# Splitting x from a turned host copy, with the first norm's row factor put on the projections

## The chip, the cores and the metric

One core of a Trainium2 chip runs the whole program. The time is the device time of one execution in microseconds (us), taken as the median of several runs. Engines: PE multiplies matrices into PSUM, DVE (VectorE), ACT (ScalarE) and POOL (GpSimd) do elementwise work, SP issues transfers. Each works through its own list of instructions in order and waits at semaphores.

## The reference, cut to what matters

Two sequences of 512 tokens (1024 tokens, D_MODEL 1024) go through one encoder layer. The first norm and the projections that read it are what is changed:

```python
def rms_norm(x, g):
    y = xf * lax.rsqrt(jnp.mean(xf * xf, axis=-1, keepdims=True) + EPS)
    return (y * g).astype(x.dtype)

h = rms_norm(x, ln1_gain)
q, k, v, u, g_attn, g_ssm = split(h @ w_in)      # six projections
```

u (1024 columns) goes into the state-space branch: blocks of 8 steps, 64 groups of 16 channels, a scan over 64 chunks in both directions. g_attn and g_ssm (1024 columns each) are gates and pass a sigmoid. q and k pass a norm over each head of 64 (q * rsqrt(mean q^2 + EPS)) and go, with v, into a windowed attention. An MLP follows. The row factor rsqrt(mean x^2 + EPS) is one number for each token, the gain is one number for each of the 1024 input columns.

All arithmetic is fp32. A product of two fp32 operands is made as three PE products: each operand is split into a high part (ACT rounds it to the PE's fp32r) and a low part (DVE subtracts), and hi*hi, hi*lo and lo*hi are added in PSUM.

## The kernel before, in words

The normed x is held as hT: for each sequence (of two, index s) a tile of 128 partitions (columns of x within a block) x 8 blocks k x 512 tokens, high and low part (the tiles act). To make it, the front loads x by rows, 8 tiles `xt` of 128 tokens x 1024 columns; ACT squares a tile with a sum over its row (L297), POOL adds EPS and takes the power -0.5, DVE multiplies the row tile by that factor (L303, 8 instructions of 128x1024). For each (s, k) PE turns four 128x128 pieces into one PSUM bank (L308), ACT writes the high part times the gain from that bank, DVE the low part (L311).

**Columns.** The 24 blocks of 128 columns (8 u, 8 g_attn, 8 g_ssm) each have a weight of 128x8x128, loaded by SP in halves (c_raw) one block ahead and split by ACT (c_hi, L175) and DVE (c_lo, L176). A block makes two *products*, one for each sequence: 24 matmuls of 128x512 into one of three PSUM banks (acc, L185). ACT then takes the bank into a tile of both sequences (128x1024, tag ev, two buffers): u with a rearrangement, gates by a sigmoid (L202), or by a copy late in the program. ACT's queue stores the tile to DRAM (u_scr, ga_scr, gs_scr). Then follow 8 key products (L225), normed at once, which stay in two ev tiles and are moved to the attention's tile kn by two transfers.

**Fillers.** All these products come from one generator. The other stages call pull(units) and thereby put the next matmuls of the generator into the PE order between their own (a matmul counts 2 units, one of a key product 1). The order of each engine is thus written out by hand in the front and the tables, and for PE, ACT and DVE in the later stages too; there POOL and SP are ordered by a scheduler. What a stage pulls is the same before and after except in the front.

**Stages in order.** The *front*: x, its split, the first products, and some hundred small DVE instructions on 128x64 tiles (exponentials and sines for the step sizes). The *tables*: for 16 quarters, DVE builds tables of powers, PE turns them (L524) and multiplies them with u and with each other (L553), while columns are pulled. Sums of lags go to lag_scr. The *scan*: 62 steps on DVE, four instructions of 128x256 each on two SBUF operands (L621 to L624), pull(15) after each. The *states*: after the scan 128 groups of PE products on u and on the Toeplitz blocks (L655) and on the states, in 8 batches whose operands (u_sb, toep, ctab) POOL's queue loads. toep comes from toep_scr, which POOL's queue fills from lag_scr by 8 transfers (L595) before the scan. Then keys, gated linear unit, attention, output product, MLP.

The lines most spoken of:

```python
V.tensor_mul(t1, h[:, i], a8r)              # a step of the scan, L621 to L624
V.tensor_mul(t2, h[:, i, ::-1], a8i)
V.tensor_add(t1, t1, h[:, i + 1])
V.tensor_add(h[:, i + 1], t1, t2)
pull(15)
```

## Time and profile before

| | us |
|---|---|
| three runs | 1472.97, 1475.15, 1476.32 (median 1475.15) |
| span of the profiled execution | 1471.1 |
| first turn of a table (end of the front) | 55.84 |
| first step of the scan on DVE | 213.13 |
| last step of the scan on DVE | 324.21 |
| states end, keys begin | 404.50 |
| PE busy | 1442.0 (98%) |
| DVE busy | 1092.2 (74%) |
| ACT busy | 754.9 (51%) |
| POOL busy | 226.8 (15%) |

The first column of a row in the chain of waits or in a timeline is the time in us at which the work began, the second how long it took. A group of instructions is shown as line, engine, operation, output<-inputs, shape, count, then the busy time in us and the mean of one in ns, then the idle time ahead of it and what ended most of it. Where a line's instructions are listed with three figures (270/272/421) these are the shortest, the middle and the longest in ns, followed by the time from the first to the last. The stages show DVE in turn as the fuller or the emptier neighbour of PE, so each is read by itself.

### The profile page before, as it was taken

To read this page: it belongs to the slowest core of one execution; us is meant where nothing else is said; L and a number is where in the kernel's file an instruction comes from. 1 tells how busy PE (TensorE), PEld (TensorE's weight loads), DVE (VectorE), ACT (ScalarE), POOL (GpSimd) and SP (SyncE) were. 2 spreads that over 40 slices of the span, in tenths; PEclk is the share of its full clock that TensorE was granted. 3 is DMA by queue.
4 is the path that set the end of the run, shared out by engine and by line. 5 is a ranking of instruction groups with operands and counts; after the bars stand their busy time and mean duration, and the time that the engine had idled before them with its cause. 6 is when DMAs were issued, how large, how long until landed. Compare 5 with 4: busy or idle time off the path is not lost.

```text
span 1471.1 us, 22069 instructions
## 1 busy us (share of the span) xinstructions
PE 1442.0 (98%) x8074; PEld 1230.7 (84%) x8074; DVE 1092.2 (74%) x1965; ACT 754.9 (51%) x1346; POOL 226.8 (15%) x372
## 2 busy tenths in 40 slices
PE   6999999999999999999999999999999999999998
PEld 4888888888999999987888878888888878888787
DVE  7989849995446899988985587777776597475553
ACT  6678852234336888786343355454454444333332
POOL 3044451003332442252100000000000000000000
PEclk9999999999999999999999999999999999999999
DMA  4455559428630533345552255444442993454441
GB/s 177 137 165 174 159 157 339 144 100 288 234 135 24 172 104 106 105 150 177 182 192 102 86 169 174 149 146 154 145 146 108 339 330 103 158 184 147 126 130 58
DMA packets 98269, 234.48 MB, mean 159 GB/s; under 512 B 11722, under 2 KB 23242, under 8 KB 98160
## 3 DMA queue, kind: packets, MB, share of 16 engines
q1 hardware_dynamic: 59088, 135.35, 28.5%
q0 software_dynamic: 15744, 47.23, 9.9%
q10 hardware_dynamic: 23328, 50.47, 9.4%
q8 instruction: 64, 1.05, 0.3%
q14 instruction: 45, 0.37, 0.1%
HBM read 163.78 MB, written 80.77 MB: 166 GB/s over the span
## 4 chain that ended last, share of the span: by engine, by line
PE 74%; DVE 12%; DMA 4%; issue 4%; ACT 4%; POOL 2%; SPq 0%; DVEq 0%; ACTq 0%; POOLq 0%
PE bank L117 14%; PE bank L118 13%; PE bank L116 13%; PE acc L185 6%; PE acc L821 5%; PE acc L117 3%; PE acc L118 3%; PE acc L116 3%; PE acc L123 2%; DMA c_raw<-in_w_ug_dram 2%; PE sps L553 2%; PE po L904 2%; PE sps L872 2%; PE tps L888 2%; PE acc L225 1%
## 5 line engine op out<-in xcount | busy, mean ns | idle before, releaser
L185 PE MATMUL acc<-act,c_hi 128*128 128x512 f32 x768 | 244.2, 396 | 1.0 <-DVE act L311 1.0
L117 PE MATMUL bank<-b_lo,a_hi 128*128 128x512 f32 x448 | 174.6, 390 | 2.3 <-DVE b_lo L1515 2.3
L118 PE MATMUL bank<-b_hi,a_lo 128*128 128x512 f32 x448 | 174.3, 389 | 0.0
L116 PE MATMUL bank<-b_hi,a_hi 128*128 128x512 f32 x448 | 173.5, 389 | 0.0
L185 PEld LDWEIGHTS acc<-act,c_hi 128*128 128x128 f32 x768 | 143.0, 189 | 30.4 <-DVE act L311 2.4
L1514 ACT CAST a_hi<-d_a 128x1024 fp32r<-128x1024 f32 x56 | 59.0, 1054 | 180.5 <-PE bank L117 177.1
L185 PE MATMUL acc<-act,c_lo 128*128 128x512 f32 x384 | 151.0, 393 | 0.0
L116 PE MATMUL bank<-act,act 128*128 128x512 f32 x368 | 143.3, 389 | 0.5 <-ACT f_sum L1339 0.5
L117 PE MATMUL bank<-act,act 128*128 128x512 f32 x368 | 143.3, 389 | 0.2 <-DVE act L1298 0.2
L118 PE MATMUL bank<-act,act 128*128 128x512 f32 x368 | 143.2, 389 | 0.0
L1515 DVE TENSOR_TENSOR a_lo<-d_a,a_hi 128x1024 fp32r<-128x1024 f32 x56 | 68.5, 1224 | 98.5 <-ACT a_hi L1514 98.5
L821 PE MATMUL acc<-w_hi,act 128*128 128x256 f32 x512 | 114.1, 291 | 0.0
L117 PEld LDWEIGHTS bank<-b_lo,a_hi 128*128 128x128 f32 x448 | 84.1, 188 | 20.7 <-DVE b_lo L1515 3.3
L116 PEld LDWEIGHTS bank<-b_hi,a_hi 128*128 128x128 f32 x448 | 84.1, 188 | 17.6
L118 PEld LDWEIGHTS bank<-b_hi,a_lo 128*128 128x128 f32 x448 | 84.1, 188 | 17.4
L821 PEld LDWEIGHTS acc<-w_hi,act 128*128 128x128 f32 x512 | 87.1, 190 | 3.7
L185 PEld LDWEIGHTS acc<-act,c_lo 128*128 128x128 f32 x384 | 72.3, 188 | 14.7 <-DVE c_lo L176 0.4
L882 ACT ACTIVATE p<-p,nmx 128x257 f32<-128x257 f32 (+1 forms) x128 | 72.1, 564 | 19.7 <-DVE nmx L876 17.6
L116 PEld LDWEIGHTS bank<-act,act 128*128 128x128 f32 x368 | 69.1, 188 | 15.4 <-ACT f_sum L1339 0.9
L117 PEld LDWEIGHTS bank<-act,act 128*128 128x128 f32 x368 | 69.1, 188 | 14.8 <-DVE act L1298 0.5
L123 PE MATMUL acc<-act,gc_hi 128*128 128x512 f32 x256 | 81.2, 394 | 0.0
L118 PEld LDWEIGHTS bank<-act,act 128*128 128x128 f32 x368 | 69.1, 188 | 14.2
(333 smaller groups left out, 3425.1 us busy)
## 6 DMA issues: line engine op xcount, KB each, us to landing
d_a<-a_scr SPq DMA_DIRECT2D x56, 512.0 KB, 3.8
raws<-in_w_up_dram SPq DMA_DIRECT2D x32, 512.0 KB, 4.0
a_scr<-t ACTq DMA_DIRECT2D x64, 256.0 KB, 2.9
k<-in_w_down_dram SPq DMA_DIRECT2D x32, 512.0 KB, 5.9
c_raw<-in_w_ug_dram SPq DMA_DIRECT2D x48, 256.0 KB, 3.8
ct_scr<-ctab POOLq DMA_DIRECT2D x16, 512.0 KB, 4.7
ctab_in<-ct_scr POOLq DMA_DIRECT2D x16, 512.0 KB, 7.3
a_scr<-a ACTq DMA_DIRECT2D x32, 256.0 KB, 2.0
```

The source lines that it names most:

```text
L116: PE.matmul(ps, a[0], b[0], start=first, stop=False)
L117: PE.matmul(ps, a[0], b[1], start=False, stop=False)
L118: PE.matmul(ps, a[1], b[0], start=False, stop=last)
L123: PE.matmul(ps, w[wi][:, k, :], rows[yi], start=k + p == 0, stop=k == KT - 1 and p == 2)
L185: PE.matmul(ps, w[wi][:, k, :], hT[s][hi][:, k, :], start=n == 0, stop=n == 3 * KT - 1)
L553: PE.matmul(ps[:, i * P:(i + 1) * P], bm[:, ri, g, :], u_sb[:, gp * SH + g, :], start=True, stop=True)
L821: PE.matmul(self.ps, hT[sq][act][:, k, col:col + P], w[:, k % 4, :], start=i == 0, stop=i == 3 * KT - 1)
L872: PE.matmul(ps[:, 0:self.nk], qs, kk[:, self.k0 * P:self.k1 * P], start=i == 0, stop=i == 1)
L882: S.activation(p, p, AF.Exp, bias=self.nmx[:, h:h + 1], scale=-1.0, accum_out=self.sums[:, h, self.qb:self.qb + 1])
L888: PE.transpose(pt[:, h * P:(h + 1) * P], self.p[:, h, 1 + i * P:1 + (i + 1) * P], ident)
L1514: S.copy(hi, src)
L1515: V.tensor_sub(lo, src, hi.bitcast(F32))
```

## The change

The host gives x a second time, turned (x_t: sequence, block of columns, 128 columns, 512 tokens). The front loads these 16 blocks (256 KB each) and ACT and DVE split them times the gain straight from SBUF. The row factor is left out of hT, so every product that reads hT comes out without it. x is still loaded by rows, 4 buffers, only to be squared with a row sum: in turn on ACT (L346) and on DVE (L348). POOL makes the four factors of each token column (rs_all) and EPS times (mean x^2 + EPS) (eps_all). DVE multiplies the identity by each column of factors (diag, L357), PE multiplies that by a tile of ones (L362), and ACT's copy of the result (rsb, 128x512 for each sequence, the factor of a token in each of the 128 partitions) is what the products are multiplied by (put_out):

- u: DVE multiplies from PSUM with the rearrangement (L187), ACT's queue stores it for one sequence at a time.
- gates in the front and the tables: DVE multiplies from PSUM (L204), ACT does the sigmoid in place.
- gates in the scan: ACT copies the bank, POOL multiplies by rsb in SBUF (L200), ACT's sigmoid and store follow when 13 matmuls of the next product have been issued (flush_later).
- gates in the states: DVE multiplies and the product is stored.
- keys and queries: their head norm takes eps_all in place of EPS, so that the factor cancels. v: rs_all is a per-partition scale as it leaves PSUM (v_evac).

Products that end before the factors are there keep their banks and are taken out later (owed, pay). The first two products run side by side over the blocks k as these land (first_products_of). A buffer of ev is now 128x512, for one sequence; kn is filled in place, without the two transfers. The front pulls more: 193 matmuls of columns stand before the first turn of a table where 130 stood.

```diff
...
+    def put_out(i, ps, s):
+        kind, blk = columns[i]
+        dst = evh.tile([P, HALF], F32, tag="ev", name="up" if kind == "u" else "sg")
+        if kind == "u":
+            V.tensor_mul(dst.rearrange("p (t k) -> p t k", t=T), ps.rearrange("p (k t) -> p t k", t=T),
+                         rsb[s].rearrange("p (k t) -> p t k", t=T))
+            S.dma_start(u_scr[blk * 8:(blk + 1) * 8].rearrange("g c t (s k) -> s (g c) t k", s=NSEQ)[s],
+                        dst.rearrange("p (t k) -> p t k", t=T))
+            return
+        scr = (ga_scr if kind == "a" else gs_scr)[blk - (GA_BLK if kind == "a" else GS_BLK)][:, s * HALF:(s + 1) * HALF]
+
+        def finished():
+            S.activation(dst, dst, AF.Sigmoid)
+            S.dma_start(scr, dst)
+
+        if phase["stage"] == "scan":
+            S.copy(dst, ps)
+            GP.tensor_mul(dst, dst, rsb[s])
+            phase["later"].append(finished)
+            sigmoids.add((blk, s))
+            return
+        V.tensor_mul(dst, ps, rsb[s])
+        if phase["stage"] == "states":
+            S.dma_start(scr, dst)
+        else:
+            finished()
+            sigmoids.add((blk, s))
+
+    def finish(i, ps, s):
+        if s in phase["normal"]:
+            put_out(i, ps, s)
+        else:
+            phase["owed"].append(lambda: put_out(i, ps, s))
+
+    def flush_later():
+        while phase["later"]:
+            phase["later"].pop(0)()
+
+    def products(i, s, splits=False):
         ps = acc()
+        w = loaded[i]
         for n in range(3 * KT):
             k, p = divmod(n, 3)
             wi, hi = [(0, 0), (0, 1), (1, 0)][p]
             PE.matmul(ps, w[wi][:, k, :], hT[s][hi][:, k, :], start=n == 0, stop=n == 3 * KT - 1)
             if n == 3 * KT - 1:
-                finish(ps, s)
+                finish(i, ps, s)
             if splits and n in (3, 9):
                 split(n // 6)
+            if n == 12:
+                flush_later()
             yield 2
 
-        def finish(ps, s):
-            if kind == "u":
-                S.copy(dst.rearrange("p (t s k) -> p t s k", t=T, s=NSEQ)[:, :, s, :], ps.rearrange("p (k t) -> p t k", t=T))
-            elif phase["gelu"]:
-                S.copy(dst[:, s * HALF:(s + 1) * HALF], ps)
-            else:
-                S.activation(dst[:, s * HALF:(s + 1) * HALF], ps, AF.Sigmoid)
-                sigmoids.add((blk, s))
...
+    def first_products_of(s, blocks):
+        banks = [acc() for _ in blocks]
+        for k in range(KT):
+            for i, ps in zip(blocks, banks):
+                for p, (wi, hi) in enumerate(((0, 0), (0, 1), (1, 0))):
+                    PE.matmul(ps, loaded[i][wi][:, k, :], hT[s][hi][:, k, :], start=k + p == 0,
+                              stop=k == KT - 1 and p == 2)
+                    if k == KT - 1 and p == 2:
+                        finish(i, ps, s)
+                    yield 2
...
+        yield from first_products_of(0, (0, 1))
+        yield from products(0, 1)
+        yield from products(1, 1, True)
         for i in range(2, len(columns)):
+            for s in range(NSEQ):
+                yield from products(i, s, s == 0)
...
-        def scale_rows(t):
-            V.tensor_scalar_mul(xs[t], xs[t], scales[t])
...
+        def split_block(s, k):
+            h = hT[s][0][:, k, :]
+            S.activation(h, xk[s, k], AF.Copy, scale=gain_1[:, k:k + 1])
+            V.scalar_tensor_tensor(hT[s][1][:, k, :], xk[s, k], gain_1[:, k:k + 1], h.bitcast(F32),
+                                   op0=ALU.mult, op1=ALU.subtract)
+        def square_row(t):
+            s, i = divmod(t, 4)
+            if i == 0:
+                sums[s] = small.tile([P, 4], F32, tag="ss", name="ss")
+            if i % 2 == 0:
+                S.activation(rows[t], rows[t], AF.Square, scale=D ** -0.5, accum_out=sums[s][:, i:i + 1])
+            else:
+                V.tensor_tensor_reduce(rows[t], rows[t], rows[t], 1.0 / D, 0.0, ALU.mult, ALU.add, sums[s][:, i:i + 1])
+        def factors(s):
+            ss, rs = sums[s], rs_all[:, s * 4:s * 4 + 4]
             GP.tensor_scalar_add(ss, ss, EPS)
+            GP.tensor_tensor(rs, ss, neg_half[:, 0:4], op=ALU.pow)
+            GP.tensor_scalar_mul(eps_all[:, s * 4:s * 4 + 4], ss, EPS)
+            diags[s] = xin.tile([P, 4, P], F32, tag="diag", name="diag", bufs=1)
             for i in range(4):
+                V.tensor_scalar_mul(diags[s][:, i], ident, rs[:, i:i + 1])
+        def spread_factors(s):
+            ps = ps_o.tile([P, 512], F32, tag="po", name="spread")
+            for i in range(4):
+                PE.matmul(ps[:, i * P:(i + 1) * P], ones, diags[s][:, i], start=True, stop=True)
+            S.copy(rsb[s], ps)
+            phase["normal"].add(s)
+        def pay():
+            if phase["owed"]:
+                phase["owed"].pop(0)()
...
-        some(6)
-        for t in range(4):
-            square_rows(t)
-        for t in range(4):
-            scale_rows(t)
-            some(3)
-        split(0)
-        split(1)
-        for k in range(KT):
-            turn_rows(0, k)
-            if k % 2 == 0:
-                square_rows(4 + k // 2)
-            elif k > 1:
-                scale_rows(3 + k // 2)
-            if k in (4, 5):
-                split(k - 4)
-            if k > 1:
-                pull(6)
-        scale_rows(7)
+        split_weights(0, 0)
+        split_block(0, 0)
+        split_weights(1, 0)
+        for k in range(1, KT):
+            split_block(0, k)
+            if k == 3:
+                split_weights(0, 1)
+                split_weights(1, 1)
+            pull(12)
+            if k in (4, 5, 6, 7):
+                square_row(k - 4)
+            else:
+                some(3)
         pull(12)
-        for k in range(KT):
-            turn_rows(1, k)
+        factors(0)
+        split_block(1, 0)
+        split_block(1, 1)
+        for k in range(2, KT):
+            split_block(1, k)
             pull(6)
-            some(4)
+            if k == 5:
+                spread_factors(0)
+            elif k > 5:
+                pay()
+            some(1)
+        pull(12)
+        for t in range(4, NT):
+            square_row(t)
+            some(2)
+            pull(6)
+        factors(1)
+        some(4)
+        pull(12)
+        spread_factors(1)
+        pay()
+        pull(12)
+        pay()
+        some(4)
         GP.tensor_scalar_mul(gain_q, gain_q, HD ** -0.5)
         GP.tensor_scalar_mul(nsink, nsink, -1.0)
         GP.tensor_tensor(dmask, ident[:, 0:CH], ident[:, 32:32 + CH], op=ALU.add)
...
-            phase["gelu"] = True
+            phase["stage"] = "states"
             pull(64)
+            flush_later()
...
-            S.copy(va[:, t, :, 0:HD], psv)
-            V.tensor_sub(va[:, t, :, HD:P], psv, va[:, t, :, 0:HD].bitcast(F32))
+            S.activation(va[:, t, :, 0:HD], psv, AF.Copy, scale=rs_all[:, t:t + 1])
+            V.scalar_tensor_tensor(va[:, t, :, HD:P], psv, rs_all[:, t:t + 1], va[:, t, :, 0:HD].bitcast(F32),
+                                   op0=ALU.mult, op1=ALU.subtract)
...
-                GP.tensor_scalar_add(ms, ms, EPS)
+                tok = self.key[1] * 4 + self.t
+                GP.tensor_scalar_add(ms, ms, eps_all[:, tok:tok + 1])
...
```

Three places where the order of the instructions moves. First DVE in the front. Before, row scalings (L303, xt) stand between the small instructions on the step sizes (ex_q, dt):

```order
9 L339 TENSOR_SCALAR ex_q<-ex_r 128x64
10 L303 TENSOR_SCALAR xt<-xt,rs 128x1024
11 L340 TENSOR_TENSOR ex_q<-ex_q,ex_r 128x64
12 L342 SCALAR_TENSOR_TENSOR ex_q<-ex_q,ex_r 128x64 x2
16 L343 TENSOR_SCALAR ex_q<-ex_q 128x64
```

After, the splits of x (L338, from xt in SBUF), squares (L348), factors spread on the identity (L357) and the first two products of u on their way out (L187):

```order
23 L338 SCALAR_TENSOR_TENSOR act_104<-xt,vec,act_103 128x512 x2
24 L348 ISA rows,ss<-rows 128x1024
25 L348 ISA ss 128x1
26 L357 TENSOR_SCALAR diag<-ident,vec 128x128 x4
27 L338 SCALAR_TENSOR_TENSOR act_106<-xt,vec,act_105 128x512 x3
28 L414 SCALAR_TENSOR_TENSOR ex_q<-ex_q,ex_r 128x64
35 L338 SCALAR_TENSOR_TENSOR act_106<-xt,vec,act_105 128x512
36 L187 TENSOR_TENSOR up<-acc,rsb_116 128x512
37 L417 TENSOR_SCALAR ex_i<-ex_n 128x64
```

The small instructions now come behind the splits of the first sequence, and squares and products stand among them.

Second, POOL around the scan. Before, the fill of toep_scr, the loads of the states' operands and the store of line (line_scr, a table for the attention's bias) follow each other:

```order
138 L579 DMA lag_scr<-ks 16x2x16
139 L595 DMA toep_scr<-lag_scr 16x64x128 x8
140 L601 DMA u_sb<-u_scr 128x8x128
141 L603 DMA toep<-toep_scr 128x1024
142 L609 DMA ctab_in<-ct_scr 128x1024 x3
145 L616 DMA line_scr<-line_one 2048x1x512
```

After, multiplies of gates (L200) stand between them:

```order
129 L200 TENSOR_TENSOR sg<-sg,rsb_117 128x512
130 L683 DMA toep_scr<-lag_scr 16x64x128 x8
131 L689 DMA u_sb<-u_scr 128x8x128
132 L200 TENSOR_TENSOR sg<-sg,rsb_116 128x512
133 L691 DMA toep<-toep_scr 128x1024
134 L697 DMA ctab_in<-ct_scr 128x1024 x3
137 L704 DMA line_scr<-line_one 2048x1x512
138 L200 TENSOR_TENSOR sg<-sg,rsb_117 128x512
```

One multiply comes ahead of the fill of toep_scr, one ahead of the load that waits for it, and the third behind the store of line; 18 more follow in a row.

Third, ACT in the scan. Before, a pair of weight splits, two sigmoids from PSUM and a store by turns:

```order
234 L175 CAST c_hi<-c_raw 128x512 x2
235 L202 ACTIVATE sg<-acc 128x512 x2
236 L209 DMA ga_scr<-sg 128x1024
```

After, each gate is a copy from PSUM, and the sigmoid of a gate stands ahead of the copy of the next:

```order
230 L178 CAST c_hi<-c_raw 128x512 x2
231 L195 ACTIVATE sg<-sg 128x512
232 L196 DMA ga_scr<-sg 128x512
233 L199 COPY sg<-acc 128x512
237 L178 CAST c_hi<-c_raw 128x512 x2
```

The sigmoid L195 takes what POOL's L200 wrote, so ACT's place in its list now depends on POOL's.

120 lines of the change are left out of this document (59 added, 61 removed).

## The prediction

> **What bounds the kernel now.** I read the page first (span, chain), then the chain in order of time, then windows for each stage.
>
> ```profile
> span 1471.1 us, 22069 instructions
> PE 74%; DVE 12%; DMA 4%; issue 4%; ACT 4%; POOL 2%; SPq 0%; DVEq 0%; ACTq 0%; POOLq 0%
> ...
> 55.84 0.87 PE tps L524 x6
> ...
> 211.16 1.61 DMA lag_scr<-ks
> ...
> 404.50 11.05 PE acc L225 x92
> ```
>
> The span lies 4 us under the median of 1475.15, and 1.9 to 5.2 under the three runs; I add what the change does to the span to the median. The chain gives four stages that the edit can reach: the front up to the first turn of a table (55.84), the tables, the scan, the states (to 404.5). From there on the instructions are nearly the same.
>
> ```profile
> 0.00:20.00 20.00, 8.74 (x36) 6.74 (x37) 12.32 (x35) 13.25 (x22) 8.10 (x22) 1.00 0.81 299
> 20.00:40.00 20.00, 18.70 (x97) 13.74 (x96) 17.52 (x53) 11.61 (x22) 4.13 (x10) 1.00 0.09 29
> 40.00:60.00 20.00, 19.69 (x90) 15.83 (x89) 19.18 (x47) 14.78 (x37) 0.88 (x2) 1.00 0.36 119
> 100.00:120.00 20.00, 20.00 (x178) 17.61 (x178) 17.59 (x36) 15.51 (x23) 7.81 (x14) 1.00 0.59 181
> 213.00:325.00 112.00, 112.00 (x496) 92.78 (x495) 106.00 (x269) 25.16 (x43) 11.64 (x16) 1.00 0.60 207
> ```
>
> Columns: window, then busy us of PE, PEld, DVE, ACT, POOL, granted clock, DMA share, GB/s. PE idles only in the first 20 us; from 20 to 60 DVE is as full as PE. In the scan both are full: 496 products in 112 us are 0.226 us each, and DVE runs
>
> ```profile
> 213.13 0.43 DVE L621 TENSOR_TENSOR t<-h,a8r 128x256 f32<-128x256 f32 x1 [7.54 <-DMA lag_scr<-ks]
> 214.72 0.42 DVE L621 TENSOR_TENSOR t<-h,a8r 128x256 f32<-128x256 f32 x1
> 324.21 0.42 DVE L624 TENSOR_TENSOR h<-t,t 128x256 f32<-128x256 f32 x1
> L176 DVE TENSOR_TENSOR c_lo<-c_raw,c_hi 128x512 fp32r<-128x512 f32 x22 | 14.3, 685 | 2.0 <-ACT c_hi L175 2.0
> ```
>
> one step each 1.59 us (213.13 to 214.72); 62 steps are 98.6, and with the 22 weight splits between them the 111.5 us from 213.13 to 324.6 are filled, with 2.0 us of waiting. So whatever delays DVE there delays the scan's end, and the states wait for that.
>
> **The front.** Removed: 64 turns on PE, 8 row scalings on DVE. Kept: the 16 splits of x on each of ACT and DVE, now from SBUF. Added: 10 more DVE instructions of a size with the trace (below), and more products ahead of the tables: by the order of instructions 193 stand before the first turn of a table instead of 130. The 63 extra are 63 x 0.226 = 14.2 us of PE work, taken out of the states.
>
> ```profile
> L308 PE MATMUL tps<-ident,xt x32: 270/272/421, 12.9 to 34.3; 128*128 128x128 f32 x32
> 17.89 0.60 PE L308 MATMUL sps<-ident,xt 128*128 128x128 f32 x4
> L303 DVE TENSOR_SCALAR xt<-xt,rs 128x1024 f32<-128x1024 f32 x8 | 5.9, 750 | 1.4 <-POOL rs L300 1.4
> L876 DVE CUSTOM_DVE_ANT_0 p<-sps,bias,vec 128x384 f32<-128x384 f32 x64 | 38.4, 602 | 1.0 <-PE sps L872 0.5
> L876 DVE CUSTOM_DVE_ANT_0 p<-sps,bias,vec 128x256 f32<-128x256 f32 x64 | 30.5, 478 | 3.4 <-PE sps L872 3.0
> L718 DVE TENSOR_TENSOR yy<-act,act 128x512 f32<-128x512 f32 x16 | 18.4, 1152 | 0.0
> 4.98 0.20 DVE L334 TENSOR_SCALAR ex_r<-lam_sb 128x64 f32<-128x64 f32 x1 [3.96 <-DMA lam_sb<-in_lam_dram]
> 4.79 1.06 ACT L297 ACTIVATE rn_junk<-xt 128x1024 f32<-128x1024 f32 x1 [1.59 <-DMA xt<-in_x_dram]
> L719 DVE TENSOR_TENSOR gs<-gs,yy x16: 691/693/696, 688.2 to 756.5; 128x512 f32<-128x512 f32 x16
> ```
>
> Four turns took 0.60 us, so PE loses at most 16 x 0.60 = 9.6 us, most of it in time in which it waited. DVE decides. Its new work ahead of the first table: 4 squares with a sum (128 elements more cost 602 - 478 = 124 ns, so 1024 take about 602 + 5 x 124 = 1.22 us each, an estimate: 4.9), 8 evacuations of u (0.69 to 1.15 each: L719 is the plain form, L718 the one with a 32-byte stride on one side, as here in the inputs; I take 0.8: 6.4), 8 diagonals (between the 0.2 of a 64-wide row and a quarter of 0.75; 0.2: 1.6), 2 more weight splits (1.4). Sum 14.3, less 8 x 0.75 = 6.0: +8.3 (7.4 to 11.1). In the first 60 us DVE was busy 12.3 + 17.5 + 19.2 = 49.0, and its idle part was the start, when x had not landed; that part stays: x and its turned copy are 8 MB, with weights 9.7, which at 299 GB/s are down at 33 us. Nothing covers the 8.3, so the first table moves from 55.8 to about 64 (60 to 67). PE agrees: 193 x 0.226 = 43.6, 8 small products with ones about 2, a start near 6 us (the first rows of x are down at 4.79) and a few us of waiting for late rows and factors give 60 or so. **Front: +8, with 14.2 us of work done ahead.**
>
> **The tables.** Each product leaves PSUM by DVE (0.69 to 1.15) instead of ACT. Of 20 us DVE used 17.6 (window 100 to 120); 178 instructions hold some 2.2 products more, +1.5 to +2.5 us. That is 19.1 to 20.1 of 20: covered, just. About 0.75 of a pair of tables stays free, and DVE's order has no room for a late piece. **+1.5 (0 to +4).** The stores of u in 256-byte pieces use DMA engines that are 0.59 busy; I take nothing.
>
> **The scan.** Here 20 of 21 products go to POOL: a copy from PSUM on ACT, then a 128x512 multiply by the factors in SBUF. ACT was busy 25 of 112 and has room. POOL was empty, but its multiply reads SBUF while DVE does. The attention shows that pair, twice in each direction:
>
> ```profile
> L965 POOL TENSOR_TENSOR act<-act,act x8: 1288/1298/1686, 632.6 to 656.5; 128x512 fp32r<-128x512 f32 x8
> 639.71 1.29 POOL L965 TENSOR_TENSOR act<-act,act 128x512 fp32r<-128x512 f32 x1 [1.65 <-ACT act L964]
> 641.59 1.64 POOL L965 TENSOR_TENSOR act<-act,act 128x512 fp32r<-128x512 f32 x1 [0.58 <-ACT act L964]
> 640.76 1.32 DVE L949 TENSOR_TENSOR ya<-ya,gate 128x1024 f32<-128x1024 f32 x1
> L949 DVE TENSOR_TENSOR ya<-ya,gate x8: 1161/1215/1322, 499.4 to 685.9; 128x1024 f32<-128x1024 f32 x8
> 647.45 1.29 POOL L965 TENSOR_TENSOR act<-act,act 128x512 fp32r<-128x512 f32 x1 [2.66 <-ACT act L964]
> 648.50 1.33 DVE L953 TENSOR_TENSOR ya<-ya,fac 128x1024 f32<-128x1024 f32 x1
> 649.28 1.69 POOL L965 TENSOR_TENSOR act<-act,act 128x512 fp32r<-128x512 f32 x1 [0.54 <-ACT act L964]
> ```
>
> DVE's L949 starts 0.24 before POOL ends (641.00) and is 0.11 longer than its median. POOL's next one starts 0.49 before L949 ends (642.08) and is 0.35 longer than 1.29. L953 and the last row repeat it (0.24 and 0.11; 0.55 and 0.40). Each loses its overlap less about 0.14, whatever the overlap: one waits for the other's end, they do not share. L949 has two inputs in SBUF, as all four instructions of a scan step have. So a multiply of 1.29 in a DVE that never pauses costs DVE about 1.29 - 2 x 0.14 = 1.0 us. Twenty of them: 20, less the 2.0 of waiting that DVE has. Bounds: 0 (they fit in gaps) and 20 x 1.29 = 25.8. **+18**, the lower bound being kept as a rival. PE waits for weight splits and the last state; behind the scan stand the states.
>
> POOL's queue brings a second delay. Its loads for the states stand in order between the multiplies: the second multiply comes before the load of toep, the third behind the store of line.
>
> ```profile
> 213.30 6.08 POOL L595 DMA_DIRECT2D toep_scr<-lag_scr  x8 [1.64 <-DMA lag_scr<-ks]
> 233.64 0.57 POOL L603 DMA_DIRECT2D toep<-toep_scr  x1 [13.35 <-DMA toep_scr<-lag_scr]
> 237.86 1.07 POOL L616 DMA_DIRECT2D line_scr<-line_one  x1
> ```
>
> POOL stood 13.35 us for toep_scr and issued line at 237.86 to 238.93. On this clock the third product is ready near 222 (products run from before 213, 24 x 0.226 = 5.4 each), its multiply runs at 239 to 240. ACT stands at its sigmoid from about 224; queued behind are the copies of the fourth and fifth product and the first halves of a pair of weight splits, then free near 245 (three ACT pieces and a store before a buffer is free again). DVE wants these for its split behind 16 steps: 213.1 + 16 x 1.59 + 4 x 0.69 + 2 multiplies = 243. **+2 (0 to +5).** From then on POOL's queue holds multiplies alone.
>
> The Trainium skill ("SBUF — State Buffer", section "Who interferes with whom") says that a DVE instruction with two SBUF inputs contends with a GpSimd one that reads SBUF, and that the later one blocks for the whole instruction. The trace agrees (0.35 us lost of 0.49). No run here shows it in an unbroken row of DVE instructions.
>
> **The states.** 63 products fewer are interleaved: at most -14.2. Not all of it comes back:
>
> ```profile
> 345.00:355.00 10.00, 10.00 (x72) 9.08 (x71) 6.74 (x9) 5.50 (x10) 3.73 (x5) 1.00 0.98 333
> 375.00:385.00 10.00, 8.15 (x71) 7.94 (x70) 6.84 (x11) 3.84 (x7) 5.74 (x7) 1.00 0.95 340
> 374.49 10.68 DMA toep<-toep_scr
> L655 PE MATMUL sps<-u_sb,toep x128: 270/275/422, 325.0 to 403.8; 128*128 128x128 f32 x128
> ```
>
> The DMA engines are 0.95 and more busy at 333 to 340 GB/s, and once PE waits for a load. From 325.0 to 403.8 eight batches take 9.9 us each. Without the fillers' 14.2 PE needs 8.1; the first two and the last are free to go at that pace, the others wait for loads at perhaps 8.5. That is 3 x 1.8 + 5 x 1.4 = 12.4. **-12 (-14 to -7).** Keys go straight to their tile, without the two transfers: -0.5.
>
> Sum: +8 + 1.5 + 18 + 2 - 12 - 0.5 = +17: **1492 us**.
>
> **Rivals.**
> (1) POOL's multiplies cost DVE nothing: then the late splits find DVE with 2 us to spare, and 1475 + 8 + 1.5 - 12 - 0.5 = 1472, on the border of faster. For it: POOL idles 100 of 112 us and no row shows a long block. Against it: four overlaps with one loss.
> (2) The front is cheaper: DVE's waits at the start absorb the new work and the table starts at 58, and blocking costs half: 1475 + 2 + 1 + 9 - 13 - 0.5 = 1473.5. Against: DVE was at 88 and 96% from 20 to 60.
> (3) Slower still, one mechanism: the strided factors make all evacuations 1.15 us, DVE becomes the bound of the tables (20.1 of 20, +4) and the front gets 2.8 more, with the states returning 9: 1475 + 11 + 4 + 18 + 2 - 9 - 0.5 = 1500.5. It decides from about 1.1 us for each evacuation. The Trainium skill (same page, section "Door 1: The DMA port swizzle") says that each step to another 16-byte line is paid for; L718 agrees for a written stride (1152 against 693).
>
> **How the numbers follow.** Forecast 0.60 (1483 to 1499), rival 1 0.19, rival 2 0.11, rival 3 0.10. A measurement tells 0.2%, or 3 us. Faster: two thirds of rival 1, a third of rival 2 and what the forecast's bounds leave, about 0.21; the same 0.13; slower 0.66. The range of 8 in 10 reaches down to cover rival 1 with the front at its cheap end (1472 - 4) and up to rival 3: 1468 to 1502.
>
> **What would show it.** First table's turn near 64; squares L348 about 1.2, evacuations L187 0.7 to 1.15; in the scan DVE rows beside L200 of about 1.4 instead of 0.42, the scan some 132 us long and PE idle by some 20 there; ACT's third sigmoid in the scan about 15 us late; the states near 67. I am wrong if the scan takes 112 again, if the table starts under 58, or if the states stay at 79.

## The result, and the profile after

The changed kernel takes 1523.41 us (median of 4 runs, 1522.19 to 1524.24) against 1474.06 for the kernel before in the same comparison: a ratio of 1.0346, interval 1.033 to 1.0361. It is 49 us slower. The prediction was 1492, with a range of 1468 to 1502: the sign was right, the size a third of what came.

The page and the chain of waits of the changed kernel (chain: share of the span by engine, then single pieces: start, us, what):

```profile
span 1521.3 us, 22106 instructions
PE 71%; DVE 13%; issue 5%; DMA 5%; ACT 3%; POOL 3%; ACTq 0%; SPq 0%; POOLq 0%; DVEq 0%
...
61.87 0.26 ACT er L528
62.15 3.57 DMA bcx<-in_coefs_dram
...
71.36 1.94 PE tps L610 x8
```

The first turn of a table comes at 71.36, not 55.84. The windows (window, busy us of PE, PEld, DVE, ACT, POOL, clock, DMA share, GB/s) of the front, of a stretch of tables, of the scan, of the states' first groups and of the other groups:

```profile
0.00:20.00 20.00, 12.57 (x45) 9.85 (x46) 11.92 (x28) 12.40 (x20) 2.99 (x10) 1.00 0.93 331
20.00:40.00 20.00, 14.48 (x55) 10.10 (x53) 14.46 (x36) 8.31 (x16) 3.25 (x5) 0.91 0.64 217
60.00:80.00 20.00, 14.99 (x60) 12.03 (x59) 16.25 (x31) 8.74 (x28) 1.30 (x2) 0.83 0.55 153
120.00:140.00 20.00, 20.00 (x178) 17.61 (x177) 20.00 (x39) 14.91 (x21) 7.82 (x14) 1.00 0.61 170
234.77:371.86 137.09, 121.39 (x504) 95.74 (x502) 127.31 (x269) 36.37 (x61) 39.27 (x36) 0.96 0.49 167
371.86:381.93 10.07, 6.47 (x28) 6.05 (x29) 6.65 (x11) 4.19 (x6) 0.23 (x1) 0.66 0.25 79
381.93:448.48 66.55, 58.25 (x472) 56.99 (x471) 36.70 (x53) 26.98 (x49) 28.36 (x33) 0.95 0.82 280
```

In the front PE is now less busy than before from 20 to 40 (14.48 against 18.70), and so is DVE (14.46 against 17.52): neither is full. The windows of the whole front, after and before:

```profile
0.00:71.36 71.36, 52.74 (x211) 40.16 (x212) 54.21 (x145) 34.21 (x67) 8.97 (x23) 0.97 0.64 205
0.00:55.17 55.17, 42.60 (x196) 32.65 (x197) 44.19 (x126) 35.40 (x65) 12.54 (x33) 1.00 0.44 157
```

DVE is busy 10.0 us longer and idle 6.2 us longer (17.15 against 10.98). Of its waits there, 4.0 us are for ACT's splits of x, 2.9 for POOL's factors and 1.7 for the load of bcx; in the kernel before, the waits of the same kinds were 1.6, 1.4 and none. In the tables (120 to 140) both are at 20.00 of 20. In the scan PE is idle 15.7 us of 137.1. PE's granted clock is under 1.00 in five of the seven windows of the stages, 0.66 at the lowest.

Where the 50.2 us between the two spans lie, from the times of the first or last instruction of each stage (us, after less before): front up to the first turn 55.17 to 71.36, **+16.2** (the instruction itself starts at 55.17, the chain's piece at 55.84); tables to the last PE product on u 145.6 to 152.7, **+7.1**; from there to the scan's first step 12.3 to 10.7, **-1.6**; scan 111.5 to 137.1, **+25.6**; scan's end to the ninth group of the states 6.9 to 10.1, **+3.1**; the other groups 72.5 to 66.6, **-6.0**; keys **-0.5**; from the last key to the end 1055.6 to 1061.85, **+6.3**.

The scan shows POOL and DVE in the same rows (timeline of both, start and us):

```profile
274.90 1.56 POOL L200 TENSOR_TENSOR sg<-sg,rsb 128x512 f32<-128x512 f32 x1 [2.54 <-ACT sg L199]
275.22 1.51 DVE L711 TENSOR_TENSOR t<-h,a8i 128x256 f32<-128x256 f32 x1
276.66 0.41 DVE L712 TENSOR_TENSOR t<-t,h 128x256 f32<-128x256 f32 x1
281.15 1.50 POOL L200 TENSOR_TENSOR sg<-sg,rsb 128x512 f32<-128x512 f32 x1 [4.70 <-ACT sg L199]
281.42 1.51 DVE L712 TENSOR_TENSOR t<-t,h 128x256 f32<-128x256 f32 x1
L200 POOL TENSOR_TENSOR sg<-sg,rsb x21: 1263/1300/1614, 233.4 to 362.6; 128x512 f32<-128x512 f32 x21
```

One DVE instruction beside a multiply takes 1.4 to 1.5 us instead of 0.42 (a weight split 1.75 instead of 0.68). The 21st multiply lies just ahead of the scan. Of the 20 in it, 17 cost DVE 0.97 to 1.12 us each, from one DVE start to the next. The other three: the one at 242.10 lies behind POOL's load of u, and the two together cost 1.79; the one at 263.74 runs as DVE falls idle; the one at 271.07 meets a weight split that came late, and costs 0.68. POOL's store of line, right ahead of a multiply, costs 0.97 as well. POOL's queue and ACT behind it:

```profile
255.18 0.60 POOL L691 DMA_DIRECT2D toep<-toep_scr  x1 [11.78 <-DMA toep_scr<-lag_scr]
259.39 1.07 POOL L704 DMA_DIRECT2D line_scr<-line_one  x1
260.47 1.49 POOL L200 TENSOR_TENSOR sg<-sg,rsb 128x512 f32<-128x512 f32 x1
261.99 0.63 ACT L195 ACTIVATE sg<-sg 128x512 f32<-128x512 f32 x1 [8.60 <-POOL sg L200]
270.40 0.59 ACT L199 COPY sg<-acc 128x512 f32<-128x512 f32 x1 [4.73 <-DMA ga_scr<-sg]
270.89 1.14 ACT L178 CAST c_hi<-c_raw 128x512 fp32r<-128x512 f32 x2
271.54 1.36 DVE L179 TENSOR_TENSOR c_lo<-c_raw,c_hi 128x512 fp32r<-128x512 f32 x1 [6.25 <-PE acc L227]
```

POOL stands 11.78 us for toep_scr, its third multiply runs at 260.5, ACT stands 8.60 us for it, then 4.73 for the store that frees a buffer, and DVE stands 6.25 us for its weight split. (The profile names PE as its releaser; the piece that came last by ACT's list is c_hi at 270.89.) From one DVE start to the next this gap is 7.3 us longer than usual. That is the delay that the prediction put at 2.

### The profile page after: what moved, and what is told of

It is laid out like the page before. It is cut to its first block, busy times and chain, and to the rows that moved or that the text cites. A ratio compares the mean times of both kernels' runs of the same rounds, so it can differ in the third digit from the quotient of the medians.

```text
span 1521.3 us, 22106 instructions
## 1 busy us (share of the span) xinstructions
PE 1455.6 (96%) x8026; PEld 1236.7 (81%) x8026; DVE 1136.8 (75%) x2001; ACT 754.2 (50%) x1340; POOL 256.0 (17%) x383
## 4 chain that ended last, share of the span: by engine, by line
PE 71%; DVE 13%; issue 5%; DMA 5%; ACT 3%; POOL 3%; ACTq 0%; SPq 0%; POOLq 0%; DVEq 0%
PE bank L118 13%; PE bank L119 13%; PE bank L117 13%; PE acc L227 6%; PE acc L914 5%; PE acc L118 3%; PE acc L119 2%; PE acc L117 2%; PE acc L124 2%; PE po L998 2%; PE sps L639 2%; PE sps L966 2%; PE tps L982 2%; DMA toep<-toep_scr 1%; DMA toep_scr<-lag_scr 1%
## 5 line engine op out<-in xcount | busy, mean ns | idle before, releaser
L227 PE MATMUL acc<-act,c_hi 128*128 128x512 f32 x736 | 237.3, 402 | 9.1 <-ACT sg L199 4.4
L119 PEld LDWEIGHTS bank<-b_hi,a_lo 128*128 128x128 f32 x448 | 84.1, 188 | 17.4
L117 PEld LDWEIGHTS bank<-b_hi,a_hi 128*128 128x128 f32 x448 | 84.1, 188 | 17.4
```

The costliest lines, as they stand in the source:

```text
L117: PE.matmul(ps, a[0], b[0], start=first, stop=False)
L119: PE.matmul(ps, a[1], b[0], start=False, stop=last)
L227: PE.matmul(ps, w[wi][:, k, :], hT[s][hi][:, k, :], start=n == 0, stop=n == 3 * KT - 1)
```

## The experiments

Stages in us, as defined above (front; tables; scan; first groups; other groups; last key to the end). They are read from one profiled execution of each kernel. The ratios are to runs of the kernel before made in the same comparison, whose medians lay between 1471.8 and 1474.1:

| kernel | front | tables | scan | first | others | end | median | ratio to before |
|---|---|---|---|---|---|---|---|---|
| before | 55.2 | 145.6 | 111.5 | 6.9 | 72.5 | 1055.6 | 1474.1 | |
| after | 71.4 | 152.7 | 137.1 | 10.1 | 66.6 | 1061.9 | 1523.4 | 1.0346 |
| scan_raw | 72.2 | 149.4 | 108.1 | 9.0 | 64.9 | 1061.9 | 1492.8 | 1.0140 (1.0107 to 1.0174) |
| scan_dve | 70.7 | 152.8 | 117.6 | 10.0 | 68.2 | 1061.9 | 1502.8 | 1.0203 (1.0178 to 1.0229) |
| scan_first3 | 70.5 | 149.3 | 129.1 | 10.4 | 66.0 | 1062.0 | 1512.8 | 1.0273 (1.0246 to 1.0300) |
| pool_twice | 70.8 | 151.6 | 162.1 | 9.2 | 66.2 | 1061.7 | 1544.3 | 1.0490 (1.0470 to 1.0511) |
| fewer_ahead | 70.9 | 149.1 | 138.3 | 11.3 | 71.7 | 1057.8 | 1523.0 | 1.0339 (1.0313 to 1.0364) |
| before_ahead | 69.3 | 148.1 | 108.4 | 7.9 | 64.7 | 1062.1 | 1486.0 | 1.0090 (1.0073 to 1.0107) |
| ring | 71.0 | 152.6 | 137.3 | 7.6 | 63.8 | 1056.7 | 1516.7 | 1.0300 (1.0278 to 1.0323) |
| sc_low | 70.3 | 152.0 | 137.8 | 10.2 | 65.9 | 1062.5 | 1521.8 | 1.0335 (1.0320 to 1.0351) |
| coefs_early | 74.0 | 149.0 | 138.7 | 9.6 | 66.7 | 1062.0 | 1522.6 | 1.0342 (1.0325 to 1.0360) |
| sc_low_coefs | 75.1 | 148.4 | 137.5 | 9.2 | 65.0 | 1062.6 | 1520.6 | 1.0324 (1.0308 to 1.0341) |
| coefs_130 | 69.2 | 148.9 | 138.9 | 10.9 | 73.2 | 1057.0 | 1522.1 | 1.0337 (1.0321 to 1.0353) |
| best | 66.8 | 148.4 | 119.6 | 10.1 | 73.2 | 1058.5 | 1502.4 | 1.0210 (1.0190 to 1.0230) |
| one_factor | 66.3 | 148.9 | 137.1 | 10.6 | 70.3 | 1055.5 | 1514.4 | 1.0295 (1.0277 to 1.0312) |
| no_factor | 60.5 | 148.1 | 138.0 | 11.5 | 71.0 | 1056.5 | 1511.7 | 1.0281 (1.0262 to 1.0300) |
| plain_out | 57.9 | 145.6 | 110.2 | 6.9 | 73.4 | 1056.6 | 1475.4 | 1.0025 (1.0015 to 1.0036) |

### The scan: four ways of multiplying

scan_raw, in which a gate in the scan leaves as before, without its factor:

```diff
-            S.copy(dst, ps)
-            GP.tensor_mul(dst, dst, rsb[s])
-            phase["later"].append(finished)
+            S.activation(dst, ps, AF.Sigmoid)
+            S.dma_start(scr, dst)
```

> The changed kernel, but the gates that leave PSUM in the scan pass ACT's sigmoid straight from PSUM: no copy, no multiply on POOL. Left out: the row factor of these 20 gate products. Theory (each POOL multiply takes 1.1 us from DVE, and one wait behind POOL's queue takes 7): the scan goes from 137.1 us back to 112 to 114, the total from 1523 to about 1497. Rival (the scan is slow for another reason, such as a PE clock that dips after its waits, or late weights): the scan stays over 125, the total over 1510.

scan_dve puts `V.tensor_mul(dst, ps, rsb[s])` in place of the copy and POOL's multiply:

> The changed kernel, but DVE multiplies the gates of the scan from PSUM, so POOL has no multiplies. Theory: each product costs DVE its own 0.65 us in place of 1.08, and the wait behind POOL's queue is gone: the scan is 111.5 + 20 x 0.65 - 2 = 122 to 124, the total about 1509. Rival (a full DVE pays the same wherever the multiply stands): the scan stays near 137, the total near 1523.

scan_first3 does so for the first three gates alone:

> The changed kernel, but the first three gates of the scan are multiplied by DVE from PSUM; from the fourth on POOL does them. Theory: the 7.3 us in which DVE stands for a weight split come from the third multiply, which waits in POOL's queue behind the loads; they go, and three gates cost 0.65 in place of 1.08: the scan is about 130, the total about 1516. Rival (the split waits for a late weight load, not for ACT behind POOL): the scan stays at 136 to 137, the total at 1522.

pool_twice repeats the line `GP.tensor_mul(dst, dst, rsb[s])`:

> The changed kernel in which POOL multiplies each gate of the scan twice by the factor (the outputs of these 20 gates then hold its square). Theory (each POOL multiply shuts DVE out for its length): the scan grows by another 20 x 1.1, to 157 to 161, the total to 1543 to 1548. Rival (what DVE loses is the changeover, or the wait for ACT, not the multiply's length): the scan stays under 146, the total under 1533.

All four sided with the theory against its rival. The sizes were not all met: the scans of scan_raw and scan_dve are 4 us below the ranges given, that of pool_twice 1 us above. The windows of the scan in scan_raw, scan_dve and pool_twice:

```profile
233.37:341.48 108.11, 108.11 (x479) 89.52 (x478) 104.58 (x269) 23.61 (x40) 11.63 (x16) 1.00 0.61 209
```

```profile
234.24:351.80 117.56, 115.39 (x504) 93.80 (x502) 114.72 (x289) 24.19 (x40) 11.63 (x16) 1.00 0.56 193
```

```profile
233.00:395.00 162.00, 128.37 (x509) 100.47 (x507) 147.06 (x268) 36.27 (x62) 69.45 (x58) 0.91 0.41 141
```

Without the multiplies the scan takes 108.1, so they cost 29.0. The same work on DVE costs 9.5 (117.6 less 108.1), 0.47 for each product: the instruction takes 0.68 us, and part of that goes into waits between the steps. The 29.0 can be read from DVE's row, by how much later than in scan_raw each instruction follows the one ahead of it: 20.7 beside 19 of the multiplies, 1.0 beside the store of line, and 7.3 in the one gap.

In pool_twice the scan is 25.0 longer again. By the same reading the multiplies now cost 42.6, about 1.04 for each of the 21 that were added, and the one gap is 11.5. So DVE loses 1.0 to 1.1 of a multiply's 1.3 us each time, also when two follow each other; the rest of the 25.0 is the longer wait behind POOL's queue. In scan_first3 the gap of 7.3 is gone, which is most of the 8.0 that this scan is shorter; the cheaper multiplies are the other 0.7.

### What 63 matmuls ahead of the tables are worth

fewer_ahead is the changed kernel with `pull(2)`, and before_ahead the kernel before with `pull(254)`, in place of `pull(128)` ahead of the tables.

> The changed kernel, but 63 matmuls fewer are pulled ahead of the tables (130 as before, not 193). Theory (DVE sets the front and loads set the states, so the 63 buy little): the first table at 69 to 71 in place of 71.4, the end of the tables 4 us nearer (u's last load is no longer behind a weight load), the states 5 to 8 us longer, the MLP 5 us shorter (the first product there gets another PSUM bank): total 1515 to 1521. Rival (the 14.2 us done ahead come back in the states): total 1528 to 1535.

> The kernel before with 63 matmuls more pulled ahead of the first table (193, as in the change), nothing else. The prediction said that such work comes back by 12 us in the states. Theory now (loads pace the states, and a queue and a PSUM ring are shifted): the front is 14 us longer, since PE does them there, the states are only 3 to 7 us shorter, and the stretch after the keys is 4 to 6 us longer by the bank ring: total 1482 to 1490. Rival (the work comes back): total 1472 to 1476.

In the changed kernel the 63 make no difference in the total: 1523.0 lies between the ranges of theory (1515 to 1521) and rival (1528 to 1535), and fits neither. The front is as long without them: it does not wait for PE, which then stands 17.4 us ahead of the first turn where it stood 5.0. Without them the states are 6.4 longer and the scan 1.2, but the tables are 3.6 shorter and the end 4.0. In the kernel before they cost 14.1 in the front, where PE is full, and bring 3.1 in the scan and 6.8 in the states; the tables and the end take back 2.5 and 6.5; the total of 1486.0 lies within the theory's range. In the states PE waits for loads of toep: 8.3 us in five waits in the changed kernel, 3.5 in fewer_ahead, 2.9 in the kernel before. That is why they do not get shorter by all that is taken out of them.

The tables' 3.6 lie at their end. From the last eight turns to the last product on u the changed kernel takes 10.7, fewer_ahead 7.1, the kernel before 6.2. One part is SP's list (SP's and PE's timeline of the changed kernel):

```profile
212.46 1.60 SPq L168 DMA_DIRECT2D c_raw<-in_w_ug_dram  x2
214.16 0.44 SPq L631 DMA_DIRECT2D u_sb<-u_scr  x1
220.39 1.83 PE L639 MATMUL sps<-u_sb,bm 128*128 128x128 f32 x7 [3.22 <-DMA u_sb<-u_scr]
```

The last load of u stands behind a pair of weight loads that wait for a split, and PE waits 3.22 us for it. With 130 matmuls ahead the pair comes after it, and PE waits 1.3. The other part is PE's clock, which is halved behind the longer wait (see the tables below).

### The end: a ring of three PSUM banks

The first product of the MLP's main part takes PSUM bank 0. By the addresses in the two built programs, bank 0 was last held by the first of two products ahead of it in the kernel before, and by the second in the changed one, since 63 matmuls more ahead shift where the tables take their banks out of the ring of three. PE's timeline, first in the kernel before, then in the changed one:

```profile
865.18 0.50 PE L116 MATMUL bank<-act,act 128*128 128x512 f32 x1 [0.50 <-ACT f_sum L1339]
908.33 0.39 PE L119 MATMUL acc<-act,act 128*128 128x512 f32 x1
912.98 0.49 PE L117 MATMUL bank<-act,act 128*128 128x512 f32 x1 [4.27 <-DVE f_sum L1430]
913.69 0.63 PE L119 MATMUL bank<-act,act 128*128 128x512 f32 x1
```

```diff
+        PE.transpose(acc()[:, 0:P], ident, ident)
         for _ in first_products(ws):
```

> The changed kernel with one 128x128 turn into an acc bank ahead of the first two products of the MLP, which shifts the ring of three PSUM banks by one. Its result is not used. Theory: the first MLP product behind them again gets the bank that ACT empties early, and PE no longer stands 4.3 us for DVE: the stretch from the last key to the end is 1056 to 1058 in place of 1061.9, the total about 1518. Rival (PE waits there for DVE's work itself): 1061 to 1062, total 1523.

The end takes 1056.65 in place of 1061.85, and the product (timeline of PE in ring) no longer waits for f_sum:

```profile
903.88 0.50 PE L117 MATMUL bank<-act,act 128*128 128x512 f32 x1
905.02 0.50 PE L118 MATMUL bank<-act,act 128*128 128x512 f32 x1 [0.65 <-DVE act L1391]
```

So 5.2 of the 6.3 us go with the place in the ring. fewer_ahead and coefs_130 (1057.8, 1057.0) have the old place in the ring, before_ahead (1062.1) has the new one. The total fell by 6.7 in the medians. In the profiled execution the states, too, are 5.3 shorter. The edit does not touch them; the windows of their first and other groups in ring show a clock of 1.00 where the changed kernel had 0.66 and 0.95:

```profile
371.51:379.06 7.55, 4.84 (x33) 4.28 (x33) 6.68 (x11) 4.19 (x6) 0.23 (x1) 1.00 0.33 105
379.06:442.87 63.81, 55.50 (x472) 54.22 (x471) 36.74 (x53) 26.94 (x49) 28.32 (x33) 1.00 0.86 292
```

PE is busy 55.50 us for the same 472 instructions that took 58.25.

### The front

Addresses in the built program show that the first bcx now overlaps the tile of powers pi (bytes 114,656 to 116,704 and 114,208 to 116,512), since the pool of x grew; hence 62.15 in the chain above. sc_low opens the two pools in the other order: bcx then lies on row tiles, and is down at 53.7. coefs_early raises the counts of small DVE instructions, `some(3)`, `some(1)` and `some(2)`, to `some(6)`, lets those of the first blocks run also at squares, and pulls 194 units where 128 stood, so that 193 matmuls stay ahead. sc_low_coefs does both; coefs_130 is coefs_early with `pull(68)`.

> The changed kernel with its two front pools opened in the other order, so that the first load of bcx no longer lands on the tile of powers (pi), which ACT reads until 62.1. Theory: bcx is down before DVE asks for it, the 3.6 us of that load leave the front: first table at 67 to 68 in place of 71.4, total about 1519. Rival (the load is covered, DVE is behind anyway): first table at 70 to 72, total 1523.

> The changed kernel, but the small DVE instructions on the step sizes are given to DVE six at a time from the first block of x on, not one to three; as many matmuls (193) ahead of the tables. Theory (DVE idles 13 us in the first 40 us, since these instructions, which it could do, stand behind squares, factors and late blocks of x): the first table at 62 to 65 in place of 71.4, total 1514 to 1517. Rival (DVE's new work fills the front, whatever its order): first table at 69 to 72, total 1521 to 1524.

> Both edits of the front together. Theory: they add up, first table at 58 to 62, total 1510 to 1514. Rival (one covers the other): the same as the better of the two alone.

> The changed kernel with the small DVE instructions given early (six at a time) and only 130 matmuls ahead of the tables. Theory (the front of the change is set by DVE's late small instructions or, once these are early, by the 63 more matmuls on PE; either alone does nothing, both together do): first table at 58 to 61, states 72, the stretch after the keys 1057, total 1508 to 1514. Rival (the new work of DVE sets the front): first table at 68 to 72, total 1520 to 1523.

All four theories fell: 70.3, 74.0, 75.1 and 69.2, where 67, 64, 60 and 60 were expected. In sc_low the load is no longer waited for, but ACT's copies of pi for the tables end 1.9 us later than in the changed kernel. In coefs_early ACT's second rsb, the factors of the second sequence, comes at 51.7 instead of 41.8. So what one edit freed was waited for elsewhere. In coefs_130 the small instructions were through by 43, and then:

```profile
46.10 1.22 DVE L348 CUSTOM_DVE_ANT_0 rows<-rows 128x1024 f32<-128x1024 f32 x1
48.11 1.05 POOL L353 TENSOR_TENSOR vec<-ss,neg_half 128x4 f32<-128x4 f32 x1
49.19 0.87 DVE L357 TENSOR_SCALAR diag<-ident,vec 128x128 f32<-128x128 f32 x4 [1.26 <-POOL vec L353]
50.82 1.05 PE L362 MATMUL spread<-diag,ones 128*128 128x128 f32 x8
51.91 0.59 ACT L363 COPY rsb<-spread 128x512 f32<-128x512 f32 x1 [4.88 <-PE spread L362]
52.53 1.15 DVE L187 TENSOR_TENSOR up<-acc,rsb 128x512 f32<-128x512 f32 x1 [2.46 <-ACT rsb L363]
```

The factors of the second sequence go through DVE, POOL, DVE, PE, ACT and DVE in turn; ACT's copies of the powers for the tables stand in its list behind this (55.8 to 61.1). So three more kernels took parts away, each on top of coefs_130: one_factor leaves out the second sequence's four row tiles and the making of its factors (both use `rsb[0]`), no_factor sets all factors to one and leaves all of their making out, plain_out also lets the products leave by ACT without a multiply.

> The early kernel with 130 matmuls ahead (coefs_130), but the second sequence takes the first one's factors: left out are its four row tiles, squares, diagonals and spread, so its outputs carry the wrong factor. Theory (the second chain of squares, POOL's power, diagonals, spread and ACT's copy stands in every engine's list ahead of the table's start): first table at 60 to 63 in place of 69.2. Rival (the loads of x or DVE's evacuations set the front): 66 to 69.

> As before, but all factors are ones: left out are the eight row tiles, squares, diagonals and spreads of both sequences (outputs without the first norm's row factor); the multiplies of the products stay. The tile of powers no longer lies under bcx. Theory: first table at 52 to 56, what is left over the kernel before in the front being DVE's evacuations of u at 1.1 us. Rival (splits and loads set the front): over 60.

> As no_factor, and the products leave PSUM by ACT as in the kernel before, without a multiply: what is left of the change is x turned by the host, no turns on PE and no row scaling. Left out is the first norm's row factor. Theory: first table at 46 to 51, scan 111, total 1462 to 1468, so the removal alone would be worth 5 to 10 us and the factor costs 55 to 60. Rival (the removed work was covered): 1470 to 1474.

66.3 and 60.5 are what the rivals had; plain_out's 57.9 is far from the theory's 46 to 51, and its total of 1475.4 lies above the theory and just above the rival's 1470 to 1474. Yet they divide the front: the second sequence's factors, with the loads of its rows, 2.9 (69.2 to 66.3), the first's 5.8 (to 60.5; this also frees the memory under bcx), evacuation by DVE 2.6 (to 57.9), and loads and splits without any factor still 2.7 more than before. The windows of the front in plain_out, and of its part up to the first turn:

```profile
0.00:20.00 20.00, 11.38 (x34) 7.93 (x35) 12.10 (x43) 9.08 (x16) 5.07 (x19) 1.00 0.92 323
20.00:40.00 20.00, 13.73 (x38) 8.57 (x36) 16.91 (x58) 6.18 (x10) 0.00 (x0) 0.76 0.14 28
0.00:57.91 57.91, 41.85 (x133) 28.93 (x133) 39.38 (x120) 26.59 (x49) 5.94 (x21) 0.88 0.46 145
```

PE, rid of the 64 turns, is busy 13.73 of 20 where it was 18.70, and at a clock of 0.76. Up to the first turn it has 63 instructions fewer than in the kernel before and is as long busy: 41.85 us against 42.60, at a clock of 0.88 instead of 1.00. So plain_out, in this order of work, gives nothing for the removal of turns and scalings: 1.0025, interval 1.0015 to 1.0036. PE's time for the turns became waiting and a lower clock.

### The edits that helped, together

best is coefs_130 with the other order of the pools and DVE's multiplies in the scan.

> All edits that helped: small DVE instructions early, 130 matmuls ahead, the other order of the two front pools, DVE multiplies the gates of the scan. Theory: first table at 57 to 60, scan 118, total 1488 to 1494, still 1% over the kernel before: what is left is the multiply on a full DVE in the scan (6 to 7 us) and DVE's work in the front. Rival: below 1480, if the parts save more together than alone.

1502.4, above what was expected: the front took 66.8, not 57 to 60, and the scan 119.6. It saves 21 us of the 49 and does not reach the kernel before; none of the kernels run does.

## Why the prediction was wrong, point by point

| term | predicted | measured in the spans |
|---|---|---|
| front | +8 | +16.2 |
| tables, to the scan's first step | +1.5 | +5.4 |
| scan | +20 | +25.6 |
| states | -12 | -2.8 |
| keys | -0.5 | -0.5 |
| the rest | 0 | +6.3 |
| sum | +17 | +50.2 |

**Front: the step failed.** "Nothing covers the 8.3, so the first table moves from 55.8 to about 64" added DVE's new durations as if DVE were the only path, and of DVE's idle time it said "that part stays". DVE's busy time grew by 10.0 and its idle time by 6.2, together the 16.2. Two sizes were right: squares 1.22 as estimated, diagonals 0.22. The 8 evacuations took 1.10 where 0.8 was taken, 2.4 in all (L187 in the listing of its line):

```profile
L187 DVE TENSOR_TENSOR up<-acc,rsb x16: 1071/1102/1186, 29.2 to 145.0; 128x512 f32<-128x512 f32 x16
```

What was left out of DVE's sum is that making the factors is a serial path over the lists of DVE, POOL, PE and ACT, at whose steps DVE stands; only PE's check had "a few us of waiting" for it. Leaving out both sequences' factors, with the loads and the memory that they use, takes 8.7 of the 14.0 that coefs_130 is over the kernel before.

**Tables: too small, and for another cause.** Of the 7.1 up to the last product on u, 2.2 lie between the first and the second table (11.3 against 9.1), 0.5 in the 14 tables after that (130.7 against 130.3) and 4.4 in the stretch behind the last turns. So evacuation by DVE, for which +1.5 was forecast, costs the tables' pace at most 0.8: with the same evacuations coefs_early takes 130.3 for those 14 and coefs_130, the slowest, 131.1. The other two lie at pauses of PE, 5.0 us ahead of the first turn and 3.2 for the last load of u, which the prediction did not look at. Behind them PE's clock is halved for a time. scan_raw has the same instructions in the tables, waits 2.9 for u, and takes 149.4. The windows of the tables in the changed kernel and in scan_raw:

```profile
71.36:224.04 152.68, 149.21 (x1238) 129.64 (x1242) 138.29 (x260) 108.64 (x158) 56.66 (x100) 0.97 0.54 157
72.23:221.67 149.44, 146.26 (x1238) 127.12 (x1242) 138.17 (x260) 108.04 (x156) 56.63 (x100) 0.99 0.55 160
```

PE is busy 2.95 us longer for the same 1238 instructions, at a clock of 0.97 instead of 0.99. Why the stretch from there to the scan is 1.6 shorter was not looked into.

**Scan: mechanism right, the sizes off.** A multiply costs about 1.1, not 1.0, and the wait behind POOL's queue 7.3, not 2. Its rows came as told (POOL behind the store of line, ACT's third sigmoid late), but the sigmoid waited 8.6 us where 15 were forecast. The 29.0 of these terms come on a scan that without them takes 108.1, which is 3.4 less than before; before_ahead shows 3.1 of that from the 63 matmuls alone. The forecast took 2.0 off instead, for DVE's waiting. The Trainium skill ("SBUF — State Buffer", section "Who interferes with whom") says of a DVE instruction with two SBUF inputs and a GpSimd one that reads SBUF that the later of the two blocks for the whole instruction. The trace agrees nearly: in an unbroken row of DVE instructions 0.97 to 1.12 us of a multiply's 1.3 are lost.

**States: the step failed.** "63 products fewer are interleaved ... -12" (they are 63 matmuls) took nearly each matmul done ahead as time won later. The other groups are 6.0 shorter; there PE waits 8.3 us for loads of toep where it waited 2.9. The first ones are 3.1 longer: PE stood 5.0 us for ACT's copy of the state (1.4 before), and the clock of these groups is 0.66. Beside the states, what the 63 gained was given back: in the kernel before they gained 9.9 there and in the scan, and 9.0 went in the tables and at the end. The keys' -0.5 came as forecast; no run tests its reason.

**The rest: not seen.** "From there on the instructions are nearly the same" is true of the instructions, not of the banks that they get. 5.2 of the 6.3 us are the ring; 1.1 stays open.

**Rivals.** The first (multiplies cost DVE nothing) and the second (a cheaper front) fell by scan_raw and by the front's 71.4. The third was near the price of an evacuation of u, 1.10 (a gate's takes 0.68), but not its effect: DVE is at 20.00 of 20 from 100 to 160 and most tables still go two in 18.6 us, as before. The range went up only to this rival; in the event all terms but the keys missed to the same side, and 6.3 came where nothing had been put.

What stays open: plain_out's front is 2.7 us longer than the front before. In its chain of waits 26 matmuls from 40.43 on take 7.82 us, 1.9 more than 26 x 0.226, at a clock of 0.77; that may be a part, but no run tells it apart. Open, too, is which order of the factors' path would be shortest; five orders gave 67 to 75.

## What to carry to other kernels

Before work is removed from an engine, look whether the path waits for it there: the removal of 64 turns from PE gave nothing here, while the factor that took the scalings' place went over four engines in turn. A multiply on POOL beside a DVE that never pauses on two SBUF operands cost DVE 1.0 to 1.1 of the multiply's 1.3 us, more than twice the 0.47 that DVE paid for doing it from PSUM itself. When a change shifts how much of an interleaved stream is done ahead, look also at what the shift does to queues and rings far away: PE stood 3.2 us for a load behind another load and 4.3 us for a PSUM bank in other hands.

## What the runs showed of the hardware that was not expected

After a pause PE can go at half pace for about 3 us. In the changed kernel some 50 matmuls of 128x512 started 0.43 us after the one ahead of them where 0.23 is usual, in six spells of 6 to 9, five of them behind a pause (4.43 us before 263.72, 4.27 before 912.98); in the kernel before there were at most two. Windows with such spells, and one behind:

```profile
264.00:268.00 4.00, 4.00 (x10) 3.13 (x11) 1.30 (x1) 0.63 (x1) 1.02 (x1) 0.50 1.02 381
913.00:917.00 4.00, 4.00 (x11) 3.17 (x12) 3.44 (x6) 1.64 (x3) 0.00 (x0) 0.57 0.20 70
917.00:921.00 4.00, 4.00 (x19) 3.31 (x18) 2.65 (x5) 1.24 (x2) 0.00 (x0) 1.00 0.00 0
```

The granted clock is 0.50 and 0.57 there and 1.00 right after. Over the span it averages 0.986, against 0.999 before: an estimated 21 us of PE's clock held back, against 1.5. Not all of it lies on the path. The spell at 913 does (8 x 0.2 = 1.6 us); in the tables, the changed kernel's PE is 2.95 us longer busy than scan_raw's with the same instructions, and in the states' other groups 2.75 us longer than ring's.

The Trainium skill ("TensorE: Matmul & The Clock Gate", section "Part 1: The HAM clock gate (the "warmup" mystery)") says that an idle window of about 3.4 us halves the PE clock and that about 3.4 us of work bring it back. The length of the spells agrees (the one at 913 from 913.3 to 916.7). Shorter pauses go both ways here: those of 1.69 us, before 31.81, and of 2.13, before 325.79, were followed by a spell, those of 2.31, before 23.56, and of 2.57, before 286.74, were not. So a wait that is added on PE can cost more than its length. That the turns also kept PE's clock up would fit the front (1.00 before, 0.88 in plain_out), but was not tested apart.
